# Order of the residual updates, of the feed-forward's down products and of three smaller pieces in a two-layer streaming encoder

## The chip, the cores and the metric

One core of one Trainium2 chip. The metric is the device time of one execution in microseconds (us). The kernel before took 3310.58 us, the median of three runs from 3303.72 to 3311.89.

## The reference, cut to what matters

Two requests run as one set of 1056 frames (1024 + 32) of width 1024 through two layers. Layer 0 mixes frames by retention and forgetting attention, layer 1 by a diagonal state space with a gate; in both, a cross-attention over 256 memory tokens and a feed-forward block follow. Each of the three branches stands between two norms:

```python
x = x + _rmsnorm(mix, g[1])
h = _rmsnorm(x, g[2])
mk, mv = _memory_kv(mem, mem_norm_w[layer], w_xk[layer], w_xv[layer])
x = x + _rmsnorm(_cross_attn(h, mk, mv, w_xq[layer], w_xo[layer]), g[3])
h = _rmsnorm(x, g[4])
x = x + _rmsnorm(_sq_relu_mlp(h, w_up[layer], w_down[layer]), g[5])

def _sq_relu_mlp(h, w_up, w_down):          # 1024 -> 4096 -> 1024
    return jnp.square(jax.nn.relu(h @ w_up)) @ w_down
```

## The kernel before

**Layout.** The width lies on the partitions as 8 tiles of 128; the frames are the free dimension, cut into groups 0, 1 and 2 of 384, 384 and 288 columns. Every large product is three matmuls (`mm3`, L72 below it): each operand is split into a high and a low part, and high by high, low by high and high by low are summed. A weight block comes by a DMA on SyncE's queue into a raw tile `wst` (four buffers, L151), ScalarE rounds it to `wh` (L153), and VectorE takes the difference `wl` (L154); `wh` and `wl` have four buffers each, and one weight block takes one of each and two `wst`.

**Feed-forward (`mlp`).** Group 2 goes first, in four steps c: eight up blocks, then a down product into all 8 output tiles in four pairs, with two loads of `wdn` to a pair. Groups 0 and 1 follow in eight steps. Step 0 is plain. From step 1 on, `seven` forms the up product of both groups from seven products on sums of their columns; one call gives four hidden tiles, in the order `c11` (group 0), `c22` (group 1), `c12` (group 1), `c21` (group 0), and a step has two calls. I call the tiles of the second call in a step c11' to c21'. A hidden tile is written twice: its high part by ScalarE (L1379), its low part by GpSimd (L1380); for c12 and c21 VectorE makes the square first (L1527). `down` then opens two output tiles at a time: all hidden tiles but the last for the first output, the same for the second, and then the last hidden tile for both. `gather` adds each result to its sum (VectorE L1416, in step 0 ScalarE L1414). Hence the boundary between `seven` and `down` stands once in each of steps 1 to 7 of both layers: 14 places.

**Updates (`update`, L261).** The residual with its norms for one group is eight parts; part k loads the old residual into `xr` (SyncE L286, four buffers), scales and adds on VectorE (L288, L289), splits the new value into `xh` (ScalarE L215) and `xl` (VectorE L216), stores it, and sums squares (ScalarE L258, GpSimd L259). After the parts, `pre_scale` sums over the partitions by small matmuls (`a<-ones_c,acc`), and `pre_row` spreads the result.

**Order.** `_Order` (`po`) is a clock that advances with the matmuls as the program is written; `later(dt, fn)` runs fn when the clock has gone dt further. It does so with a lead of 300 in the scheduler's priority, so what it issues passes ahead of other work on each engine, within its dependences. After that each engine works strictly through its own queue. The updates of groups 0 and 1 after the cross-attention (`lax`) run beside group 2's step 0.

Of the kernel before, what the change touches and what calls it, by code (L numbers as in the profile page):

```python
# [31 lines left out]
class _Order:  # L32
# [5 lines left out]

    def later(self, dt, fn):
        heapq.heappush(self.q, (self.now + dt, self.n, fn))  # L40
        self.n += 1
# [5 lines left out]
    def step(self):  # L47
        due, _, fn = heapq.heappop(self.q)
        self.now = max(self.now, due)
        with self.first():  # L50
            fn()
# [12 lines left out]
def _body(tc, A):  # L64
# [21 lines left out]
    with es:  # L86
# [174 lines left out]
        def update(o, g, ys, acc, gpost, xres, xout, last=False, row=False, scale=1.0 / 1024, half=False, r=None, lax=False, late=False, rlate=False):  # L261
# [3 lines left out]
            R = []  # L265
            d1, d2, d3, d4, dp = (10.0, 8.0, 14.0, 8.0, 10.0) if lax else (L1, L2, 25.0 if rlate else L3, L4, PU[g])
            if last and not late:
# [4 lines left out]
            def post_scale():  # L272
                rc = rstd_cols(acc, 3, scale, half, r=None if r is None else r())
                po.later(d2, lambda: add(rc))

            def add(rc):
# [4 lines left out]
                def part(k):  # L281
# [17 lines left out]
                    if k < 7:  # L299
                        po.later(dp, lambda: part(k + 1))  # L300
                        return
# [3 lines left out]
                    if not last:  # L305
                        po.later(d3, lambda: pre_scale(acc2))

# [16 lines left out]
            def pre_scale(acc2):  # L324
                rc = rstd_cols(acc2, 3, 1.0 / 1024, tag="rc" if row else "rx", ps=ba())
                if row:
                    po.later(d4, lambda: pre_row(rc))
                else:
                    o["r"] = rc
# [5 lines left out]

            po.later(d1, post_scale)

# [36 lines left out]
        def memory_k(l, xg=0):  # L374
# [3 lines left out]
            for k in range(8):  # L378
                mt = npl.tile([128, 384], F32, tag="xr", bufs=4, name="mt")[:, :256]
                dma(mt, A["memt"][:, k, :])  # L380
                mh.append(xtile(xg, "mh")[:, :256])
                ml.append(xtile(xg, "ml")[:, :256])
                with tc.high_priority(offset=HQ):
                    split_to(mh[k], ml[k], mt, gall[:, 12 + l, k : k + 1])
# [987 lines left out]
        def mlp(l, X, out, done, gpre, xsrc, last):  # L1372
# [23 lines left out]

            def down(ws, H, os_, g):

                n = len(H)
                pss = [bank()[:, : NG[g]] for _ in os_]  # L1400
                for ks in (range(n - 1), (n - 1,)):
                    for o, ps in zip(os_, pss):
                        for k in ks:
                            wh, wl = ws[k // 4]
                            s = slice((k % 4) * 256 + (o % 2) * 128, (k % 4) * 256 + (o % 2) * 128 + 128)
                            mm3(ps, wh[:, s], wl[:, s], H[k][0], H[k][1], k == 0, k == n - 1)
                            po.tick()
# [14 lines left out]
            for c in range(4):  # L1422
# [8 lines left out]
                for s4 in range(4):  # L1431
                    ws = [wload(A["wdn"][l, 2 * c + j, s4], 4) for j in range(2)]
                    os_ = (2 * s4, 2 * s4 + 1)
# [124 lines left out]
            for c in range(8):  # L1558
# [15 lines left out]
                ws = [wload(A["wdn"][l, c, s], 4) for s in range(4)]  # L1574
                for g in (1, 0) if c == 0 else (0, 1):
                    acc = acc_tile(NG[g]) if c == 7 else None
                    for s4 in range(4):
                        os_ = (2 * s4, 2 * s4 + 1)
                        for o, ps in zip(os_, down([ws[s4]], H[g], os_, g)):
                            gather(Y[g], o, g, ps, c == 0, acc)  # L1580
# [73 lines left out]
        def s5_block(f, u):  # L1654
# [54 lines left out]
            def outputs(xg):  # L1709
# [17 lines left out]
        gemm(range(8), lambda b: wload(A["winc"][b], 8, HP if b < 2 else 0), lambda g, k: get(X, g)[k], evac_u, lambda at: 2 if at == 0 else 1,  # L1727
             post=lambda b, g: s5_block(b, uts.pop(b)) if un[b] == 3 else None, order=(2, 0, 1))
        mem = memory_k(1, 2)
# [177 lines left out]
```

## Time and profile before

| | us |
|---|---|
| median of three runs | 3310.58 |
| the profiled execution | 3306.95 |
| its span (first to last instruction) | 3305.0 |
| TensorE busy in the span | 3119.2 (94%) |
| VectorE, ScalarE, GpSimd busy | 1925.8, 1327.7, 924.7 |

The profile is one execution, on the hardware profiler. What TensorE lacks to the span is waits; a second loss does not show as idle time, matmuls that run at the lower of the clock's two levels after a wait. So a stage is read by its length, not by its busy time.

### The profile page before, as it was taken

The page shows a single profiled execution, that of the slowest core. Times are in us where ns is not written, and L with a number is a line of the kernel's source. Part 1 is how long each engine was busy: PE and PEld are TensorE (multiplying, and loading weights), DVE is VectorE, ACT ScalarE, POOL GpSimd, SP SyncE. Part 2 cuts the span into 40 slices and gives each one's busy share as a digit, 9 for nine tenths or more (in the row PEclk, how much of TensorE's full clock was granted, in tenths as well). Part 3 has the DMA queues.
Part 4 walks back from the last instruction along what each step waited for, and adds up shares of the span by engine and source line. Part 5 has one row for each costly group of instructions (what it writes and reads, how often), then busy time and mean ns, then how long its engine had stood idle before and what let it go on. Part 6 is the DMA issues. An engine that isn't in the chain of part 4 may idle for free.

```text
span 3305.0 us, 52896 instructions
## 1 busy us (share of the span) xinstructions
PE 3119.2 (94%) x19636; PEld 3009.1 (91%) x19636; DVE 1925.8 (58%) x3600; ACT 1327.7 (40%) x2801; POOL 924.7 (28%) x1182
## 2 busy tenths in 40 slices
PE   7999999998999899999999987998999899999997
PEld 7899986688999899999999887998999899999997
DVE  8853666527534756566657696217435656566565
ACT  5213344525435545433324334225435545333232
POOL 4873431216104313111114332005105212111114
PEclk9999999999999899999999898999999999999998
DMA  5462254124113655222213676214114654112113
GB/s 162 148 199 65 63 138 122 41 58 137 55 40 118 196 164 155 69 64 65 77 51 110 192 252 194 68 52 144 49 50 138 188 166 149 61 58 87 52 65 102
DMA packets 255271, 360.49 MB, mean 109 GB/s; under 512 B 42795, under 2 KB 144396, under 8 KB 254884
## 3 DMA queue, kind: packets, MB, share of 16 engines
q1 hardware_dynamic: 211222, 289.63, 28.9%
q10 hardware_dynamic: 35328, 41.83, 3.8%
q0 software_dynamic: 8464, 25.66, 2.3%
q8 instruction: 154, 2.52, 0.3%
q14 instruction: 103, 0.84, 0.1%
HBM read 294.75 MB, written 66.39 MB: 109 GB/s over the span
## 4 chain that ended last, share of the span: by engine, by line
PE 66%; DVE 7%; issue 3%; ACT 2%; POOL 2%; DMA 2%; SPq 0%; DVEq 0%; ACTq 0%; POOLq 0%
PE mm L72 59%; PE a L72 4%; PE b L72 1%; PE c L72 1%; DVE upd L289 1%; DVE upd L288 1%; POOL acc L259 1%; DVE xl L216 1%; DVE us L1527 1%; ACT wh L153 1%; PE b L76 1%; DVE wl L154 1%; POOL hm L1380 0%; DVE p L1692 0%; DVE VC L1695 0%
## 5 line engine op out<-in xcount | busy, mean ns | idle before, releaser
L72 PE MATMUL mm<-hm,wh 128*128 128x384 f32 (+1 forms) x3072 | 740.1, 326 | 33.2 <-ACT wh L153 10.4
L154 DVE TENSOR_TENSOR wl<-wst,wh 128x512 fp32r<-128x512 f32 (+1 forms) x648 | 465.5, 735 | 359.7 <-ACT wh L153 354.7
L72 PE MATMUL mm<-xh,wh 128*128 128x384 f32 x1664 | 580.9, 349 | 13.4 <-ACT mo L414 8.0
L72 PEld LDWEIGHTS mm<-hm,wh 128*128 128x128 f32 x3072 | 540.2, 190 | 42.5 <-ACT hm L1379 14.6
L72 PE MATMUL mm<-xl,wh 128*128 128x384 f32 x1664 | 567.3, 341 | 4.3 <-DVE xl L216 4.3
L72 PE MATMUL mm<-xh,wl 128*128 128x384 f32 x1664 | 566.1, 340 | 3.2 <-DVE wl L154 3.2
L153 ACT ACTIVATE wh<-wst 128x512 fp32r<-128x512 f32 (+1 forms) x648 | 390.5, 625 | 409.8 <-PE mm L72 332.6
L72 PE MATMUL mm<-hm,wl 128*128 128x384 f32 (+1 forms) x1536 | 499.0, 325 | 14.8 <-DVE wl L154 14.8
L72 PE MATMUL mm<-xc,wh 128*128 128x288 f32 (+1 forms) x2368 | 489.4, 302 | 14.6 <-DVE mo L395 8.3
L259 POOL TENSOR_TENSOR acc<-acc,sq 128x384 f32<-128x384 f32 (+2 forms) x259 | 276.7, 1074 | 483.8 <-ACT sq L258 477.4
L72 PEld LDWEIGHTS mm<-xc,wh 128*128 128x128 f32 x2368 | 387.7, 193 | 16.7 <-DVE mo L395 8.5
L72 PE MATMUL mm<-xc,wl 128*128 128x288 f32 (+1 forms) x1184 | 353.8, 299 | 3.8 <-DVE wl L154 3.8
L1380 POOL TENSOR_TENSOR hm<-us,hm 128x384 fp32r<-128x384 f32 x112 | 125.8, 1123 | 777.7 <-ACT hm L1379 752.1
L72 PEld LDWEIGHTS mm<-xh,wh 128*128 128x128 f32 x1664 | 318.3, 191 | 20.7 <-ACT mo L414 8.9
L72 PEld LDWEIGHTS mm<-xl,wh 128*128 128x128 f32 x1664 | 318.6, 191 | 5.9 <-DVE xl L216 5.9
L72 PEld LDWEIGHTS mm<-xh,wl 128*128 128x128 f32 x1664 | 317.8, 191 | 3.5 <-DVE wl L154 3.5
L72 PEld LDWEIGHTS mm<-hm,wl 128*128 128x128 f32 x1536 | 291.6, 190 | 16.0 <-DVE wl L154 16.0
L1496 ACT ACTIVATE wh<-wst 128x512 fp32r<-128x512 f32 x196 | 115.1, 625 | 418.2 <-PE mm L72 372.2
L1416 DVE TENSOR_TENSOR y<-y,mm 128x384 f32<-128x384 f32 x224 | 120.6, 554 | 232.5 <-PE mm L72 232.5
L72 PEld LDWEIGHTS mm<-xc,wl 128*128 128x128 f32 x1184 | 228.3, 193 | 4.3 <-DVE wl L154 4.3
L72 PE MATMUL mm<-T,wh 128*128 128x384 f32 x672 | 171.6, 336 | 0.0
L1497 DVE TENSOR_TENSOR wl<-wst,wh 128x512 fp32r<-128x512 f32 x196 | 136.4, 728 | 34.8 <-ACT wh L1496 34.8
(502 smaller groups left out, 5414.9 us busy)
## 6 DMA issues: line engine op xcount, KB each, us to landing
wst<-in_wup_dram SPq DMA_DIRECT2D x256, 256.0 KB
wst<-in_wdn_dram SPq DMA_DIRECT2D x256, 256.0 KB
xs<-upd ACTq DMA_DIRECT2D x80, 192.0 KB
xr<-xs SPq DMA_DIRECT2D x80, 192.0 KB
wst<-in_wab_dram SPq DMA_DIRECT2D x40, 256.0 KB
wst<-in_wxk_dram SPq DMA_DIRECT2D x32, 256.0 KB
wst<-in_wxv_dram SPq DMA_DIRECT2D x32, 256.0 KB
wst<-in_wxq_dram SPq DMA_DIRECT2D x32, 256.0 KB
```

The lines of the kernel that those rows point to most:

```text
L72: return nc.tensor.matmul(out, lhsT, rhs, **kw)
L76: return nc.tensor.transpose(out, src, idn)
L153: act(wh[:, s], st, AF.Copy)
L154: vtt(wl[:, s], st, wh[:, s].bitcast(F32), op=SUB)
L216: stt(l, src, gain, h.bitcast(F32), op0=MULT, op1=SUB)
L259: return gtt(acc[:, :n], acc[:, :n], sq[:, :n], op=ADD)
L288: stt(t, ys[k], gall[:, gpost, k : k + 1], ps[:, :n], op0=MULT, op1=MULT)
L289: (gtt if last and k % 2 or r and k < 2 or not r and (g == 2 and k % 4 == 1) else vtt)(t, t, xr, op=ADD)
L1380: gtt(lo, t, h.bitcast(F32), op=SUB)
L1416: vtt(Y[o], Y[o], ps, op=ADD)
L1496: act(wh[:, d], src, AF.Copy)
L1497: vtt(wl[:, d], src, wh[:, d].bitcast(F32), op=SUB)
```

## The change

1. `later` takes `lead`. The updates of groups 0 and 1 after the cross-attention are queued with `lead=False`: they still come at their time on the clock, but at no higher priority than the code around them. 2. Their delays change (parts every 9 instead of 10, the norm's two steps 20 and 12 after instead of 14 and 8). The norm of group 2 after the feed-forward (`late`) waits 25 and 12 instead of 5.1 and 2.7. 3. The loads of `wdn` of group 2's step 0 get a lead of 600, as its up blocks' loads have already. 4. From step 1 on, `down` takes group 1 before group 0, and for group 1 the hidden tile with index 2 (c12') last. 5. The eight tiles through which the memory tokens pass use seven buffers of three kinds instead of four of one. 6. The state-space layer's input product takes the groups in the order 2, 1, 0 instead of 2, 0, 1.

```diff
-    def later(self, dt, fn):
-        heapq.heappush(self.q, (self.now + dt, self.n, fn))
+    def later(self, dt, fn, lead=True):
+        heapq.heappush(self.q, (self.now + dt, self.n, fn, lead))
...
-        with self.first():
+        with self.first() if lead else nullcontext():
...
-            d1, d2, d3, d4, dp = (10.0, 8.0, 14.0, 8.0, 10.0) if lax else (L1, L2, 25.0 if rlate else L3, L4, PU[g])
+            d1, d2, d3, d4, dp = (10.0, 8.0, 20.0, 12.0, 9.0) if lax else (L1, L2, 25.0 if rlate or late else L3, 12.0 if late else L4, PU[g])
...
-                        po.later(dp, lambda: part(k + 1))
+                        po.later(dp, lambda: part(k + 1), not lax)
...
-                        po.later(d3, lambda: pre_scale(acc2))
+                        po.later(d3, lambda: pre_scale(acc2), not lax)
...
-                mt = npl.tile([128, 384], F32, tag="xr", bufs=4, name="mt")[:, :256]
+                tag, bufs = (("xr", 4), ("xr", 4), ("xr", 4), ("tmp", 2), ("tmp", 2), ("sqa", 2), ("sqa", 2), ("xr", 4))[k]
+                mt = npl.tile([128, 384], F32, tag=tag, bufs=bufs, name="mt")[:, :256]
...
-            def down(ws, H, os_, g):
+            def down(ws, H, os_, g, late=None):
...
+                order = [k for k in range(n) if k != late] + ([] if late is None else [late])
                 pss = [bank()[:, : NG[g]] for _ in os_]
-                for ks in (range(n - 1), (n - 1,)):
+                for ks in (order[:-1], order[-1:]):
...
-                            mm3(ps, wh[:, s], wl[:, s], H[k][0], H[k][1], k == 0, k == n - 1)
+                            mm3(ps, wh[:, s], wl[:, s], H[k][0], H[k][1], k == order[0], k == order[-1])
...
-                    ws = [wload(A["wdn"][l, 2 * c + j, s4], 4) for j in range(2)]
+                    with tc.high_priority(offset=2 * HP if c == 0 else 0):
+                        ws = [wload(A["wdn"][l, 2 * c + j, s4], 4) for j in range(2)]
...
-                for g in (1, 0) if c == 0 else (0, 1):
+                for g in (1, 0):
...
-                        for o, ps in zip(os_, down([ws[s4]], H[g], os_, g)):
+                        for o, ps in zip(os_, down([ws[s4]], H[g], os_, g, 2 if c and g == 1 else None)):
...
-             post=lambda b, g: s5_block(b, uts.pop(b)) if un[b] == 3 else None, order=(2, 0, 1))
+             post=lambda b, g: s5_block(b, uts.pop(b)) if un[b] == 3 else None, order=(2, 1, 0))
```

The line numbers of the changed kernel are one to three higher after each edit.

**Where the instructions go, first place: group 2's first down product in layer 0.** SyncE's queue, as a piece of the difference; `xr<-xs` with 384 columns is an update part's load for groups 0 and 1, `wst<-in_wdn` a down weight, `wst<-in_wup` an up weight:

```order
 L286 DMA xr<-xs_86 128x384
 L151 DMA wst<-in_wup_dram 128x512 x2
-L151 DMA wst<-in_wdn_dram 128x512 x7
+L151 DMA wst<-in_wdn_dram 128x512 x8
 L286 DMA xr<-xs_93 128x384
 L286 DMA xr<-xs_87 128x384
+L151 DMA wst<-in_wdn_dram 128x512 x2
 L286 DMA xr<-xs_94 128x384
+L151 DMA wst<-in_wdn_dram 128x512 x2
 L286 DMA xr<-xs_88 128x384
 L286 DMA xr<-xs_95 128x384
-L151 DMA wst<-in_wdn_dram 128x512
+L151 DMA wst<-in_wdn_dram 128x512 x4
```

All 16 halves of down weights now stand before the last five of the 16 residual loads, and these move in among the next step's up weights. In either layer fourteen `xr` loads stand behind the first eight halves, the last four of them group 2's own. On VectorE at the same place, of the kernel before (from the first `wl` after the last up block's hidden tile):

```order
L154 TENSOR_TENSOR wl<-wst,wh 128x512
L216 SCALAR_TENSOR_TENSOR xl<-upd,gall,xh 128x384
L289 TENSOR_TENSOR upd<-upd,xr 128x384
L216 SCALAR_TENSOR_TENSOR xl<-upd,gall,xh 128x384
L288 SCALAR_TENSOR_TENSOR upd<-y,gall,b 128x384 x2
L216 SCALAR_TENSOR_TENSOR xl<-upd,gall,xh 128x384
L289 TENSOR_TENSOR upd<-upd,xr 128x384 x2
L288 SCALAR_TENSOR_TENSOR upd<-y,gall,b 128x384 x2
L216 SCALAR_TENSOR_TENSOR xl<-upd,gall,xh 128x384
L289 TENSOR_TENSOR upd<-upd,xr 128x384 x2
L216 SCALAR_TENSOR_TENSOR xl<-upd,gall,xh 128x384
L154 TENSOR_TENSOR wl<-wst,wh 128x512
```

and of the kernel changed, the fifth to the seventh of the eight down blocks:

```order
L154 TENSOR_TENSOR wl<-wst,wh 128x512 x2
L216 SCALAR_TENSOR_TENSOR xl<-upd,gall,xh 128x384
L154 TENSOR_TENSOR wl<-wst,wh 128x512 x2
L289 TENSOR_TENSOR upd<-upd,xr 128x384
L288 SCALAR_TENSOR_TENSOR upd<-y,gall,b 128x384
L216 SCALAR_TENSOR_TENSOR xl<-upd,gall,xh 128x384
L289 TENSOR_TENSOR upd<-upd,xr 128x384
L288 SCALAR_TENSOR_TENSOR upd<-y,gall,b 128x384
L216 SCALAR_TENSOR_TENSOR xl<-upd,gall,xh 128x384
L154 TENSOR_TENSOR wl<-wst,wh 128x512 x2
L289 TENSOR_TENSOR upd<-upd,xr 128x384
L288 SCALAR_TENSOR_TENSOR upd<-y,gall,b 128x384
```

Before, 14 update instructions stood between two single halves of a weight block; now at most six stand between two whole blocks. From the last up block's hidden tile on, the changed queue has 21 update instructions and 8 halves of down weights (four blocks) up to the first up weight of the next step, and then 9 update instructions and 8 halves to the end of that step's fourth up block.

**Second place: the first pair of outputs in a step after `seven`.** TensorE, layer 0, step 1, the second output's first three hidden tiles and then the first output's last one. In the order in which they are made, the hidden tiles are 15815 (c11), 15868 (c22), 15888 (c12), 15908 (c21), 15978 (c11'), 16031 (c22'), 16051 (c12') and 16071 (c21'), each with its low part one number higher. Before:

```order
L72 MATMUL mm_16116<-hm_15815,wh_16075 128x384
L72 MATMUL mm_16116<-hm_15816,wh_16075 128x384
L72 MATMUL mm_16116<-hm_15815,wl_16076 128x384
L72 MATMUL mm_16116<-hm_15908,wh_16075 128x384
L72 MATMUL mm_16116<-hm_15909,wh_16075 128x384
L72 MATMUL mm_16116<-hm_15908,wl_16076 128x384
L72 MATMUL mm_16116<-hm_15978,wh_16075 128x384
L72 MATMUL mm_16116<-hm_15979,wh_16075 128x384
L72 MATMUL mm_16116<-hm_15978,wl_16076 128x384
L72 MATMUL mm_16115<-hm_16071,wh_16075 128x384
L72 MATMUL mm_16115<-hm_16072,wh_16075 128x384
L72 MATMUL mm_16115<-hm_16071,wl_16076 128x384
```

and changed:

```order
L72 MATMUL mm_16116<-hm_15888,wh_16075 128x384
L72 MATMUL mm_16116<-hm_15889,wh_16075 128x384
L72 MATMUL mm_16116<-hm_15888,wl_16076 128x384
L72 MATMUL mm_16116<-hm_15868,wh_16075 128x384
L72 MATMUL mm_16116<-hm_15869,wh_16075 128x384
L72 MATMUL mm_16116<-hm_15868,wl_16076 128x384
L72 MATMUL mm_16116<-hm_16031,wh_16075 128x384
L72 MATMUL mm_16116<-hm_16032,wh_16075 128x384
L72 MATMUL mm_16116<-hm_16031,wl_16076 128x384
L72 MATMUL mm_16115<-hm_16051,wh_16075 128x384
L72 MATMUL mm_16115<-hm_16052,wh_16075 128x384
L72 MATMUL mm_16115<-hm_16051,wl_16076 128x384
```

The nineteenth matmul of the product needed c21', the last tile made; now it needs c12', the last but one, and the seventh needs c22' where it needed c11'.

**Third place: the norm of group 2 after its feed-forward in layer 0.** TensorE's rows around `pre_scale`, a piece of the difference; rows on `xh` are group 1's and 0's up product in step 0, rows on `hm` their down product:

```order
+L72 MATMUL mm<-hm,wl 128x384
+L72 MATMUL mm<-hm,wh 128x384 x2
+L72 MATMUL mm<-hm,wl 128x384
 L72 MATMUL a<-ones_c,acc 128x1 x3
-L72 MATMUL mm<-xh,wh 128x384
-L72 MATMUL mm<-xl,wh 128x384
-L72 MATMUL mm<-xh,wl 128x384
```

The three small matmuls moved from inside the up product to the down product that follows it.

## Rows read from the trace of the kernel before

**Rows 1.** The page: busy time of each engine; the chain that ended last, by engine.
```profile
PE 3119.2 (94%) x19636; PEld 3009.1 (91%) x19636; DVE 1925.8 (58%) x3600; ACT 1327.7 (40%) x2801; POOL 924.7 (28%) x1182
...
PE 66%; DVE 7%; issue 3%; ACT 2%; POOL 2%; DMA 2%; SPq 0%; DVEq 0%; ACTq 0%; POOLq 0%
```

**Rows 2.** Stages of layer 0: start, end, length, busy time of each engine.
```profile
core 0: us, PE busy (x) PEld busy (x) DVE busy (x) ACT busy (x) POOL busy (x), PEclk, DMA share, GB/s
1080.73:1123.26 42.53, 30.85 (x194) 30.04 (x193) 37.39 (x54) 24.83 (x51) 17.79 (x15) 0.80 0.69 214
1251.85:1277.30 25.45, 25.45 (x194) 25.45 (x193) 13.30 (x24) 11.98 (x24) 5.71 (x6) 1.00 0.49 160
1277.30:1319.86 42.56, 39.58 (x218) 39.21 (x217) 29.26 (x56) 25.53 (x56) 19.33 (x21) 0.92 0.52 152
1319.86:1353.43 33.57, 33.57 (x193) 33.57 (x193) 16.29 (x26) 16.51 (x36) 2.66 (x2) 1.00 0.23 71
1382.80:1418.30 35.50, 34.01 (x194) 33.43 (x193) 18.21 (x31) 5.56 (x10) 2.34 (x3) 1.00 0.17 53
```

**Rows 3.** The same columns, two stages of layer 1.
```profile
2557.70:2598.99 41.29, 27.70 (x194) 27.11 (x193) 36.75 (x53) 25.54 (x52) 17.31 (x15) 0.83 0.69 211
2753.04:2787.91 34.87, 34.87 (x207) 34.87 (x206) 24.18 (x45) 18.94 (x39) 14.32 (x15) 1.00 0.52 160
```

**Rows 4.** TensorE's waits, 1350 to 1800 us (total us, times, longest).
```profile
PE mm L72 <- POOL hm L1380: 5.1, 7, 1.1
PE mm L72 <- ACT hm L1379: 5.0, 7, 0.8
```

**Rows 5.** TensorE's waits, 2826 to 3282 us.
```profile
PE mm L72 <- ACT hm L1379: 5.2, 7, 0.8
```

**Rows 6.** TensorE in order of time around one boundary (start, length, line).
```profile
1512.54 0.51 PE L72 MATMUL mm<-hm,wh 128*128 128x384 f32 x2
...
1516.56 0.44 PE L72 MATMUL mm<-hm,wh 128*128 128x384 f32 x1 [0.74 <-ACT hm L1379]
1517.67 0.44 PE L72 MATMUL mm<-hm,wh 128*128 128x384 f32 x1 [0.67 <-POOL hm L1380]
```

**Rows 7.** ScalarE and GpSimd around the same boundary, two timelines.
```profile
1513.29 0.53 ACT L1379 ACTIVATE hm<-us 128x384 fp32r<-128x384 f32 x1 [1.11 <-DVE us L1527]
...
1511.73 1.11 POOL L1380 TENSOR_TENSOR hm<-us,hm 128x384 fp32r<-128x384 f32 x1 [5.09 <-ACT hm L1379]
1513.90 1.04 POOL L1380 TENSOR_TENSOR hm<-us,hm 128x384 fp32r<-128x384 f32 x1 [1.05 <-ACT hm L1379]
1516.58 1.03 POOL L1380 TENSOR_TENSOR hm<-us,hm 128x384 fp32r<-128x384 f32 x1 [1.65 <-ACT hm L1379]
```

**Rows 8.** TensorE's waits, 1080.73 to 1123.26 us, then 2557.7 to 2598.99.
```profile
PE mm L72 <- DVE wl L154: 11.7, 3, 5.5
...
PE mm L72 <- ACT wh L153: 10.4, 1, 10.4
```

**Rows 9.** Waits of SyncE's queue, 1075 to 1123 us.
```profile
SPq L286 <- DVE upd L289: 20.2, 11, 3.2
```

**Rows 10.** VectorE's groups, 1080.73 to 1123.26 us (count, busy us, mean ns).
```profile
L154 DVE TENSOR_TENSOR wl<-wst,wh 128x512 fp32r<-128x512 f32 x19 | 13.7, 731 | 5.1 <-ACT wh L153 5.0
L289 DVE TENSOR_TENSOR upd<-upd,xr 128x384 f32<-128x384 f32 x11 | 9.9, 915 | 0.0
```

**Rows 11.** VectorE's line 289, 1076 to 1109 us (min, median, max ns).
```profile
L289 DVE TENSOR_TENSOR upd<-upd,xr x14: 546/550/1376, 1076.6 to 1108.2; 128x384 f32<-128x384 f32 x14
```

**Rows 12.** GpSimd's sums, 1080.73 to 1123.26 us.
```profile
L259 POOL TENSOR_TENSOR acc<-acc,sq 128x384 f32<-128x384 f32 x13 | 15.6, 1214 | 19.5 <-ACT sq L258 19.5
```

**Rows 13.** TensorE's waits, 1277.3 to 1319.86 us.
```profile
PE a L72 <- POOL acc L259: 3.0, 1, 3.0
```

**Rows 14.** TensorE's waits, 1960 to 1992 us.
```profile
PE mm L72 <- DVE u L1651: 5.3, 2, 3.6
```

**Rows 15.** The start of the state-space layer, columns as in rows 2.
```profile
1797.00:1860.00 63.00, 51.35 (x264) 47.96 (x263) 48.34 (x78) 26.19 (x52) 38.06 (x38) 0.84 0.57 178
```

More of the change, by code (lines that the diff above doesn't have):

```diff
@@ L8 @@
 import heapq
-from contextlib import ExitStack
+from contextlib import ExitStack, nullcontext
 import numpy as np
@@ L47, in step @@
     def step(self):
-        due, _, fn = heapq.heappop(self.q)
+        due, _, fn, lead = heapq.heappop(self.q)
         self.now = max(self.now, due)
-        with self.first():
+        with self.first() if lead else nullcontext():
             fn()
@@ L273, in post_scale @@
                 rc = rstd_cols(acc, 3, scale, half, r=None if r is None else r())
-                po.later(d2, lambda: add(rc))
+                po.later(d2, lambda: add(rc), not lax)
             def add(rc):
@@ L326, in pre_scale @@
                 if row:
-                    po.later(d4, lambda: pre_row(rc))
+                    po.later(d4, lambda: pre_row(rc), not lax)
                 else:
@@ L334, in pre_row @@
                 act(o["r"], ps[:, :384], AF.Copy)
-            po.later(d1, post_scale)
+            po.later(d1, post_scale, not lax)
         def get(out, g, key="X"):
```

## The prediction

> **What bounds the kernel now.** I read the page first: TensorE is busy 94% of the span and is 66% of the chain that ended last [rows 1], so a change pays only where TensorE waits, or runs slowly after a wait. Then I cut TensorE's work into stages and compared stages that do the same products. The same 192 matmuls of group 2's down product take 25.45 us in its last step and 42.53 us in its first, where TensorE is busy only 30.85 us and the granted clock is 0.80, while VectorE is busy 37.39 us [rows 2]; in layer 1 the first takes 41.29 us [rows 3]. A down product of the 384-column groups takes 33.57 us in step 0 and 35.50 us in step 1 [rows 2]. The waits inside these stages come last: who released TensorE, and how long it stood.
>
> **The boundary after the seven products (edit 4).** The down product starts at 1512.54; TensorE then stands 0.74 us for ScalarE's high part of the last hidden tile and 0.67 us for GpSimd's low part of it [rows 6], which ends at 1516.58 + 1.03 = 1517.61 [rows 7]. The listed waits are 5.1 + 5.0 us for seven places in layer 0 [rows 4], and the row for layer 1 has seven more of the same kind [rows 5]: about 20 us in all. The stage tells more than the list, since a matmul that follows a wait also loses its overlap with the one before: 35.50 - 33.57 = 1.93 us a place [rows 2], 27.0 us for 14.
> In the new order the tile needed first, c22', has its low part ready at 1511.73 + 1.11 = 1512.84 [rows 7]. One matmul takes 33.57 / 192 = 0.175 us, so it is wanted after six matmuls, at 1512.54 + 6 x 0.175 = 1513.59: 0.75 us to spare. c12' is ready at 1513.29 + 0.53 = 1513.82 (high) and 1513.90 + 1.04 = 1514.94 (low) [rows 7], and wanted after 18, at 1515.69: 0.75 us again. c21' now serves group 0 alone, 96 matmuls or 16.8 us later. Nothing before the boundary is moved, so these times should hold. I take **-27**; the bounds are -20 (only the listed waits come back) and -27.
>
> **Group 2's first down product (edits 1, 2, 3).** TensorE stands 11.7 us there for `wl` in layer 0 and 10.4 us in one piece for `wh` in layer 1 [rows 8]; the rest of the loss is the low clock behind those waits (0.80 and 0.83 granted on average). Why are the weights late? On SyncE's queue the residual loads wait 20.2 us in 11 waits for an update's add to free a buffer [rows 9], and the down weights stand behind them; on VectorE 14 update instructions stand between two halves of weights. Against the undisturbed 25.45 us the stages lose 42.53 - 25.45 = 17.1 and 41.29 - 25.45 = 15.8 us, together 32.9.
> The change puts all down weights ahead on both queues, but the work stays. VectorE's instructions in this stage take 37.39 / 54 = 0.69 us each, collisions included [rows 2]. In its new queue, 29 stand between the end of the up blocks and the first weights of the next step: 20.1 us against 25.45. With the 17 behind them it is 46, or 31.8 us, up to the fourth up block, which TensorE reaches at 25.45 + 3 x 3.2 = 35.0 us (an up block being an eighth of a like stage, 25.45 / 8). So VectorE fits with 3 to 5 us over, not more, and every time it waits for a freed buffer comes off that. ScalarE's 24.83 us of work in this stage [rows 2] nearly fill 25.45 too. I leave 4 us of loss in each layer, between none and half of the present one (about 8), and take **-25** (33 - 8); the bounds are -16 and -33.
>
> **Group 2's norm after its feed-forward (edit 2).** In layer 0 the three small matmuls stand inside step 0's up product and wait 3.0 us for GpSimd's sum [rows 13]; the clock falls after it, 0.92 on average. That stage takes 42.56 us, the same one in layer 1, where this norm does not exist, 34.87 [rows 2, 3]. The 7.7 us between hold the norm's own matmuls, which only move: three sums and three spreads, estimated at 1.4 us from the 218 - 207 = 11 more instructions by about 0.13 us (25.45 / 194). By the new place, more than 70 matmuls into the down product, the sum is long done. **-6.3**, bounds -3 and -7.7.
>
> **Memory tiles (edit 5).** The loads come earlier and their splits move ahead of `u` on VectorE, where TensorE already stands 5.3 us in two waits [rows 14]. One to three splits of about 0.6 us delay the second: **+1.5**, bounds 0 and +4. **State-space order (edit 6).** It only swaps two like groups where TensorE has 63.00 - 51.35 = 11.65 us idle and VectorE is busy 48.34 [rows 15]; each of several waits can move by a part of itself. **0**, bounds -3 and +3.
>
> **Sum.** -27 - 25 - 6.3 + 1.5 = -56.8 against the profiled execution's 3306.95 us gives 3250.2. That execution lies 3.6 us under the median of the runs, so for the median I say **3254 us**.
>
> **A rule against this change.** VectorE's line 289 takes 0.55 us at the median, yet 1.376 at most [rows 11], 0.915 on average in the stage [rows 10], while GpSimd runs 13 sums of 1.214 us there [rows 12]. By these rows the collisions cost 11 x (0.915 - 0.55) = 4.0 us on this line, and with the 19 `wl` at 0.731 [rows 10] they are inside the 0.69 us that I used.
> The Trainium skill, page "SBUF — State Buffer", section "SBUF: two separate sides", says that VectorE and GpSimd share one pair of ports as an exclusive lock, held for a whole instruction, and that a VectorE instruction with two inputs there fully blocks meanwhile. By that rule 13 sums pressed into a shorter stage cost VectorE up to 13 x 1.214 = 15.8 us, and the stage would hardly shrink. The longest row, 0.83 us above the median, agrees with a block by most of a GpSimd instruction; the average does not agree with a block at every one.
>
> **Rivals.** *VectorE stays the bound.* If its 37.39 and 36.75 us of work [rows 2, 3] all have to be done inside the stage, as the collisions that this rule names would have it, the losses stay 11.9 and 11.3 us, only 9.7 of 32.9 is won, and the time is 3254 + 15 = 3269. For it speaks that it was busy nearly throughout; against it, that the weights now come first and that updates can slide into the next step, whose like stage keeps VectorE busy 13.30 of 25.45 us. *The boundary wait moves on.* The margin of c12' is 0.75 us, and VectorE, ScalarE and GpSimd make it one after another; if it slips by 1.5 us, half of edit 4's gain goes: 3254 + 13 = 3267. Against it: 14 alike places, no new work ahead of them. *Slower: residual loads dam up SyncE's queue.* In each layer 14 of them now stand among down and up weights, and a load that waits for its buffer holds every weight behind it. At the 1.84 us that such a wait takes on average now (20.2 / 11) and with nothing to hide it, 28 cost 51.5 us instead of the present 32.9, and the time is 3307 - 32 + 18.6 = 3294, or 3297 for the median; at the longest wait, 3.2 us, 89.6, and it is 3332 (3335). From 64.7 / 28 = 2.3 us a load the kernel is slower than before. Against it: four blocks of weights are kept ahead, worth 4 x 3.2 = 12.7 us of matmuls. *Nothing is gained* if the waits named are only where an earlier delay shows and TensorE is held later by the same amount: 3307 to 3310. Nothing in the stages behind, which run at full clock without waits, speaks for that.
>
> **How the numbers follow.** The forecast has 0.62, VectorE as the bound 0.16, the boundary's wait 0.10, little or no gain 0.06, the dammed queue 0.06 (0.04 slower than before, 0.02 about the same). The predicted time is the forecast's. The low end takes every lower bound, -27 - 33 - 7.7 + 0 - 3 = -70.7, thus 3240; the high end takes both middle rivals at once, 3254 + 15 + 13 = 3282; 4 us more each way are for the spread of the three runs (8 us), which gives 3236 to 3286. That leaves out about 0.12 at the top and a little below. The forecast's own range is 3243 to 3266. A measurement of this kernel tells 0.3%, about 10 us, from no change: faster 0.62 + 0.16 + 0.10 = 0.88, same 0.08, slower 0.04.
>
> **What would show it.** The 14 stages after `seven` at 33.6 us with no wait on `hm`; group 2's first down products at 28 to 32 us with a granted clock near 1 and no `xr` load's wait ahead of a `wdn`; step 0's up product in layer 0 at about 35 us, with no wait for `acc`; the two waits for `u` a little longer. I am wrong if VectorE runs without a break through the first down product and TensorE still waits for `wl`; if waits for the high or low part of c12' stand at the boundary; or if the up blocks of group 2's second step begin to wait for weights.

## The result, and the profile after

The changed kernel takes 3253.43 us, the median of four runs (3251.18 to 3262.17); beside it the kernel before took 3311.23 us (four runs, 3303.72 to 3316.42). The ratio is 0.9832, with a 95% interval from 0.9806 to 0.9858: 1.7% faster, 57.8 us between the two medians. The profiled execution took 3254.24 us, its span 3252.5 us, 52.5 us less than before.

Stages first, in the columns of [rows 2]. Layer 0 of the changed kernel: group 2's first down product, the up and down product of its next step, step 0's up and down product of groups 0 and 1, and the down product of step 1.

```profile
1079.29:1106.06 26.77, 25.97 (x194) 25.50 (x193) 26.77 (x43) 19.62 (x42) 13.39 (x10) 1.00 0.81 254
1106.06:1131.79 25.73, 25.73 (x194) 25.51 (x193) 22.80 (x34) 17.96 (x39) 11.82 (x12) 1.00 0.75 241
1131.79:1158.31 26.52, 26.38 (x200) 26.15 (x199) 14.81 (x28) 11.35 (x22) 3.63 (x5) 1.00 0.55 178
1260.80:1296.55 35.75, 35.05 (x206) 34.73 (x205) 24.19 (x45) 20.12 (x44) 16.83 (x19) 1.00 0.50 142
1296.55:1338.54 41.99, 38.10 (x205) 37.27 (x205) 21.49 (x37) 22.36 (x47) 5.00 (x4) 0.92 0.29 90
1367.91:1401.48 33.57, 33.57 (x193) 33.57 (x193) 18.09 (x31) 5.56 (x10) 2.37 (x3) 1.00 0.18 57
```

Layer 1: group 2's first down product, and step 0's up and down product of groups 0 and 1.

```profile
2529.48:2556.42 26.94, 25.73 (x195) 25.50 (x193) 26.94 (x42) 19.29 (x42) 14.28 (x11) 1.00 0.81 261
2712.58:2747.44 34.86, 34.86 (x206) 34.86 (x205) 22.99 (x44) 18.18 (x38) 14.32 (x15) 1.00 0.49 153
2747.44:2787.14 39.70, 35.88 (x194) 34.94 (x193) 20.01 (x34) 21.19 (x44) 5.97 (x3) 0.96 0.28 88
```

Group 2's first down product went from 42.53 to 26.77 us and from 41.29 to 26.94, at full clock. The boundary stage went from 35.50 to 33.57, the length without any wait. Step 0's up product in layer 0 went from 42.56 to 35.75, as forecast; but the down product behind it, 33.57 us before, now takes 41.99 at a clock of 0.92. That row is the miss.

The waits of TensorE, as total, times and longest; first over all boundaries of layer 0 (1340 to 1772 us, where [rows 4] had 14 waits on `hm`):

```profile
PE mm L72 <- DVE y L1418: 0.8, 1, 0.8
```

None of the 14 is left; the one row is the last step's sum. In layer 1 (2787 to 3229 us) the same view lists nothing. Then group 2's first down product in layer 0, which answers to [rows 8]:

```profile
PE mm L72 <- ACT yc L1416: 0.7, 1, 0.7
```

and in layer 1:

```profile
PE mm L72 <- ACT yc L1416: 1.2, 1, 1.2
```

The waits for weights are gone, 11.7 and 10.4 us of them in [rows 8]; what is left waits for ScalarE to read a product out of PSUM. Then step 0's down product in layer 0:

```profile
PE mm L72 <- ACT u L1386: 3.1, 1, 3.1
PE mm L72 <- ACT y L1416: 0.8, 1, 0.8
```

and the stretch of the state-space layer where TensorE waits for `u`:

```profile
PE mm L72 <- DVE u L1654: 6.7, 2, 6.2
```

This answers to [rows 14]: 5.3 us became 6.7. SyncE's queue in the 32 us around group 2's first down product, beside [rows 9]:

```profile
SPq L286 <- DVE upd L289: 10.0, 7, 2.3
...
SPq L151 <- DVE wl L154: 10.6, 16, 2.3
```

The residual loads still wait, 10.0 us in 7 waits (to the end of the next up product 10.9 us in 8; in layer 1, from 2524 to 2586 us, 11.7 us in 8), but the weights that TensorE needs next are no longer behind them.

The account of the profiled span, from the first matmul of each stage to that of the next (us):

| stretch | before | after | difference |
|---|---|---|---|
| up to layer 0's feed-forward | 1052.6 | 1051.1 | -1.4 |
| group 2's first down product and the next step, layer 0 | 94.1 | 79.0 | -15.1 |
| the same, layer 1 | 92.9 | 80.6 | -12.2 |
| step 0 of groups 0 and 1, up and down, layer 0 | 76.1 | 77.7 | +1.6 |
| the same, layer 1 | 73.2 | 74.6 | +1.3 |
| steps 1 to 6, both layers (12 boundaries) | | | -23.0 |
| layer 1's last down product | 37.0 | 35.1 | -1.9 |
| layer 0's last down product to layer 1's feed-forward | 757.7 | 755.9 | -1.8 |

### The profile page after: what moved, and what is told of

Same layout as the page of the kernel before. It is cut to its first block, busy times and chain, and to the rows that moved or that the text cites. A ratio compares the mean times of both kernels' runs of the same rounds, so it can differ in the third digit from the quotient of the medians.

```text
span 3252.5 us, 52906 instructions
## 1 busy us (share of the span) xinstructions
PE 3107.3 (96%) x19636; PEld 3003.3 (92%) x19636; DVE 1924.5 (59%) x3600; ACT 1324.5 (41%) x2801; POOL 938.8 (29%) x1182
## 4 chain that ended last, share of the span: by engine, by line
PE 65%; DVE 6%; DMA 4%; issue 3%; ACT 2%; POOL 2%; SPq 0%; ACTq 0%; DVEq 0%; POOLq 0%
PE mm L72 58%; PE a L72 4%; PE b L72 1%; PE c L72 1%; DVE wl L154 1%; DVE upd L289 1%; POOL acc L259 1%; DVE xl L216 1%; DVE upd L288 1%; PE b L76 1%; DMA wst<-in_wxv_dram 1%; DMA yf<-yd 1%; DMA wst<-in_wup_dram 1%; DMA xs<-upd 0%; DMA xq<-xs 0%
## 5 line engine op out<-in xcount | busy, mean ns | idle before, releaser
L259 POOL TENSOR_TENSOR acc<-acc,sq 128x384 f32<-128x384 f32 (+2 forms) x259 | 283.4, 1100 | 489.9 <-ACT sq L258 483.5
```

What stands on the lines that cost most here:

```text
L259: return gtt(acc[:, :n], acc[:, :n], sq[:, :n], op=ADD)
```

## The experiments

Each is a kernel of its own, made from the kernel before or from the changed one by the edit shown. The lengths are of stages, from one profile each, counted from the first matmul of a stage to the first of the next. Where no wait stands they repeat far better than whole times, which differ by up to 16 us between runs of one kernel (edit 4 alone: 3280.41 to 3296.43).

**Edit 4 alone.** The kernel before with this and the reordered `down`:

```diff
-                for g in (1, 0) if c == 0 else (0, 1):
+                for g in (1, 0):
...
-                        for o, ps in zip(os_, down([ws[s4]], H[g], os_, g)):
+                        for o, ps in zip(os_, down([ws[s4]], H[g], os_, g, 2 if c and g == 1 else None)):
```

> The kernel before with edit 4 alone (group 1 first, c12' last). My theory: the 12 undisturbed stages after the seven products fall from 35.5 to 33.57 us, the time by 26 us to about 3285, and everything else stays, the 42.5 and 41.3 us of group 2's first down products too. Rival: half of the 52 us that the whole change gave needs the other edits as well (a shared queue), and this alone gives under 15 us.

Measured: 3285.12 us (3309.24 beside it), ratio 0.9935, 0.9915 to 0.9954. The 12 stages are at 33.57 us, group 2's first down products at 42.55 and 41.08, and the time is the forecast one. The rival falls: this term stands by itself.

**Edits 1 and 3, and edit 2 for groups 0 and 1.** The kernel before with the new `later`, the new delays of `lax` and the lead of the down weights.

```diff
-        with self.first():
+        with self.first() if lead else nullcontext():
...
-(10.0, 8.0, 14.0, 8.0, 10.0) if lax
+(10.0, 8.0, 20.0, 12.0, 9.0) if lax
...
+                    with tc.high_priority(offset=2 * HP if c == 0 else 0):
```

> The kernel before with edit 1, edit 2 for groups 0 and 1 and edit 3 (updates without lead, later norms, down weights of group 2's first step ahead), and nothing else. My theory: group 2's first down products at 27 us instead of 42.5 and 41.3, 27 us gained after what the next stages give back, about 3284 us; the wait of group 2's norm (3.0 us for the sum) is still there. Rival: without the other edits the updates' leftovers push the next stages by more than 3 us.

Measured: 3278.33 us, ratio 0.9917, 0.9895 to 0.9939. The first down products take 27.91 and 27.42 us, with the next step 80.2 and 80.8 us instead of 94.1 and 92.9: 26 us. The two stages behind them grow by 0.7 and 1.8 us, less than the rival's 3. The time is 6 us under the expected 3284, of which 3.6 us lie ahead of layer 0's feed-forward (1049.0 us instead of 1052.6), where a single profile tells little. The two parts, 26 and 26 us, make up nearly the whole of the 52.5 us between the profiles.

**Edit 3 alone, and edits 1 and 2 alone.** The same kernel split in two:

```diff
# the first: edit 3, nothing else
+                    with tc.high_priority(offset=2 * HP if c == 0 else 0):
# the second: edits 1 and 2 for groups 0 and 1, nothing else
+        with self.first() if lead else nullcontext():
...
+(10.0, 8.0, 20.0, 12.0, 9.0) if lax
```

> The kernel before with edit 3 alone: the down weights of group 2's first step get a lead of 600, the updates keep theirs of 300 and the old delays. My theory: weights late on SyncE's queue and on VectorE are the whole cause, so this alone brings the first down products to 27 to 29 us; the updates then crowd behind them and the two stages that follow (25.5 and 26.1 us) give back 1 to 4 us a layer. Rival: the lead of the updates is the cause; then the down products stay above 35 us.

> The kernel before with edit 1 and edit 2 for groups 0 and 1, without edit 3. My theory: down weights still stand behind single residual loads, no longer behind five or more; the first down products take 28 to 33 us, so either edit alone brings over half of the gain. Rival: both edits are needed, and the stages stay above 36 us.

Measured: 3286.78 and 3284.04 us, one run each. With the lead of the weights alone, in the columns of [rows 2], the first down product and the up product behind it:

```profile
1073.20:1105.26 32.06, 25.86 (x195) 25.40 (x193) 31.96 (x49) 20.93 (x46) 16.91 (x14) 1.00 0.77 246
1105.26:1134.66 29.40, 28.37 (x193) 28.02 (x193) 20.56 (x31) 17.82 (x37) 8.30 (x9) 0.88 0.61 199
```

and TensorE's waits over the two:

```profile
PE mm L72 <- ACT wh L153: 5.0, 1, 5.0
...
PE mm L72 <- DVE wl L154: 1.0, 1, 1.0
```

The down weights come in time. The wait has moved to the first up weight of the next step, which has no lead and queues behind the updates: 5.0 us, counted at the end of the 32.06 us, and the clock of the stage behind it falls to 0.88. Only 6.5 and 5.4 us are won in the two layers. With no lead for the updates and none for the weights either, the first two stages are:

```profile
1087.18:1114.04 26.86, 25.71 (x194) 25.47 (x193) 26.31 (x41) 19.79 (x41) 11.22 (x11) 1.00 0.82 254
1114.04:1140.07 26.03, 25.73 (x195) 25.49 (x194) 22.88 (x35) 18.32 (x41) 13.78 (x11) 1.00 0.71 237
```

That is the whole gain, 15.1 and 13.2 us with the down product behind; adding edit 3 to it, as in the run above, brings nothing that shows. Both of my expectations were off: I had put the cause on the place of the down weights, and it is the way the updates are queued, which push back whatever weights come next. Which part of that counts, the lost lead (edit 1) or the new delays (edit 2), is not shown: no run has one without the other. The rivals "both are needed" and "above 35 us" fall too.

**The later norm undone.** The changed kernel with

```diff
-25.0 if rlate or late else L3, 12.0 if late else L4
+25.0 if rlate else L3, L4
```

> The changed kernel with group 2's norm after its feed-forward early again (5.1 and 2.7 instead of 25 and 12). My theory of the miss: the later norm only uncovers a wait behind it, ScalarE's work on the column sums of groups 0 and 1, which step 0's up and down products of layer 0 run into. Then with the early norm the up product is back at 42 us and the down product behind it at about 34, the two together within 2 us of the 77.7 us of the changed kernel, and the time is 3252 to 3255 us. Rival: the down product is late for another reason and stays at 42 us; then the two take 84 us and the time is 3260.

Measured: 3255.14 us, ratio to before 0.9839, 0.9814 to 0.9865, against 0.9832 for the changed kernel: no difference. Step 0's up and down product, layer 0:

```profile
1263.67:1305.23 41.56, 38.35 (x219) 37.70 (x217) 30.47 (x56) 25.74 (x55) 18.56 (x21) 0.96 0.51 155
1305.23:1338.80 33.57, 33.57 (x194) 33.57 (x193) 16.30 (x26) 16.59 (x36) 2.07 (x2) 1.00 0.22 70
```

Together 75.1 us, 2.6 under the changed kernel's 77.7, a little outside the 2 us that I had allowed. Over all profiles the sign stays open: the six kernels with the early norm take 74.7 to 76.3 us for the two stages, the changed kernel and the two made from it that touch nothing here (the next two runs) 77.7, 76.9 and 74.0. So the later norm brings no gain that shows. In each of the six the down product takes 33.57 us, in all eight kernels with the later norm 39.1 to 42.0, of which the norm's own matmuls are about 1.4.

**Group 1 first, c22' last.** The changed kernel with

```diff
-down([ws[s4]], H[g], os_, g, 2 if c and g == 1 else None)
+down([ws[s4]], H[g], os_, g, None)
```

> The changed kernel with group 1 first, but its hidden tiles in their own order (c22' last instead of c12'). My theory: c12' is then wanted by the seventh matmul, 1.05 us after the start, and its low part ready 2.4 us after it, so TensorE waits for ScalarE and GpSimd again, 1.2 to 1.6 us in all, and the 14 stages take 34.9 to 35.3 us: about 20 us more in all. Rival: the order of the groups does all of it, and the stages stay at 33.57.

Measured: 3273.39 us (one run), the stages 34.88 to 34.96 us, 1.3 us above the changed kernel's. TensorE waits for the low part of c12':

```profile
PE mm L72 <- POOL hm L1381: 4.0, 6, 0.7
```

and at one of the boundaries, in order of time:

```profile
1433.91 0.45 PE L72 MATMUL mm<-hm,wh 128*128 128x384 f32 x1 [0.64 <-POOL hm L1381]
```

0.64 us are listed, 1.33 us are lost, as at the old boundary, where 1.41 listed were 1.93 lost. Of edit 4's 1.93 us the groups' order brings 0.6 and the tiles' order 1.3.

**VectorE's first instruction of each update part issued twice.**

```diff
+                    for _ in range(2 if lax else 1):
-                    stt(t, ys[k], gall[:, gpost, k : k + 1], ps[:, :n], op0=MULT, op1=MULT)
+                        stt(t, ys[k], gall[:, gpost, k : k + 1], ps[:, :n], op0=MULT, op1=MULT)
```

> The changed kernel with the first VectorE instruction of each update part of groups 0 and 1 after the cross-attention issued twice (the same result is written twice), about 0.55 to 0.6 us more for each of the 16 parts of a layer. My theory: VectorE has 3 to 5 us over in group 2's first down product and the blocks behind it, so 9 us more come out as 3 to 6 us in a layer, spread over the first down product (26.8 and 26.9 us), and the up and down products of the next step (25.7 and 26.5; 27.1 and 26.6). Rival one: VectorE is the bound already, and all 9 us come out. Rival two: ScalarE is the bound, VectorE has more room than I worked out, and less than 1.5 us comes out.

Measured: 3252.39 us (one run). The three stages, in the columns of [rows 2]:

```profile
1075.76:1101.21 25.45, 25.45 (x195) 25.45 (x193) 25.45 (x43) 18.95 (x40) 13.87 (x9) 1.00 0.82 253
1101.21:1126.67 25.46, 25.46 (x195) 25.46 (x193) 25.46 (x42) 17.41 (x37) 12.38 (x10) 1.00 0.72 234
1126.67:1158.57 31.90, 28.69 (x201) 27.80 (x199) 18.79 (x34) 13.63 (x26) 6.13 (x7) 0.95 0.53 175
```

82.8 us instead of 79.0, in layer 1 84.1 instead of 80.6: 3.8 and 3.5 us, as expected, but all of it at the third stage. The doubled line itself takes 8.9 us more in layer 0 (18.4 instead of 9.5), VectorE as a whole is busy 6.4 us more over these stages and the one ahead of them (91.2 instead of 84.8; 5.6 in layer 1), since the 64 `wl` come out shorter (736 ns on average instead of 772). VectorE is busy without a break through the first two stages, which lose nothing at all; the debt is called in at the next down product, where TensorE waits 1.8 and 1.4 us for the two parts of hidden tiles. In the whole time this does not show: the profile has other stages 2 to 4 us shorter than the changed kernel's.

**Four tries at step 0's down product.** The changed kernel with a lead for the hidden tiles of step 0, with it and one of two additions, and with the sums without lead:

```diff
# first
-H[g].append(hidden(up(ws[b], get(X, g), g), NG[g]))
+ps = up(ws[b], get(X, g), g)
+with tc.high_priority(offset=2 * HP):
+    H[g].append(hidden(ps, NG[g]))
# second: the sums alone
-po.later(1.0 + 9.0 * k, lambda k=k: sums(k))
+po.later(1.0 + 9.0 * k, lambda k=k: sums(k), False)
# third: the first, and
+po.later(1.0 + 13.0 * k, lambda k=k: sums(k))
# fourth: the first, and in gather
+with tc.high_priority(offset=HP):
+    act(Y[o], ps, AF.Copy)
```

> The changed kernel with a lead of 600 for the hidden tiles of groups 0 and 1 in step 0 (reading the product from PSUM, squaring, splitting), ahead of the column sums for the seven products, which have 300. My theory of the missed term: ScalarE reaches the last hidden tiles late because it does the column sums first, so step 0's down products (42.0 us in layer 0, 39.7 in layer 1, against 33.6 without waits) lose their first wait and with it the low clock, and fall to 36 to 38 us in layer 0 and 37 to 39 in layer 1; the time falls by 4 to 7 us to about 3248. Rival: ScalarE has too much to do in this stretch whatever its order; the wait moves to the sums or to the first step after, and nothing is gained.

> The changed kernel with the column sums for the seven products queued without lead (same times on the clock, no higher priority than the code around them), as edit 1 did for the updates. My theory: ScalarE then reads the products of step 0 out of PSUM first, and the down products fall to 35 to 37 us in both layers (from 42.0 and 39.7), with the sums still done before the first of the seven products. Rival: the sums come too late, and the stage of the first seven products (29.36 us) grows by what the down products lose.

> The changed kernel with the lead of 600 for step 0's hidden tiles and the column sums 13 instead of 9 apart on the clock. My theory: ScalarE's load in the stretch falls by a third, the last of the two waits (for the first sums that are read out of PSUM, 1.6 and 2.1 us with the lead alone) falls below 1 us, and the down products take 35 to 37 us. Rival as for the plain sums: the first seven products wait instead.

> The changed kernel with the lead of 600 for step 0's hidden tiles and as much for reading the first down products out of PSUM. My theory: both waits are matters of order on ScalarE alone, so both fall below 1 us, and the down products take 35 to 37 us in both layers. Rival: ScalarE's instructions ahead of them wait for VectorE and for loads themselves, order alone does not help, and the stages stay at 39 us as with the first lead alone.

Step 0's up and down product, and the medians (us; one run where no ratio stands):

| | layer 0 | layer 1 | time | ratio to before |
|---|---|---|---|---|
| before | 42.56 + 33.57 | 34.87 + 38.35 | 3310.58 | |
| changed | 35.75 + 41.99 | 34.86 + 39.70 | 3253.43 | 0.9832 (0.9806 to 0.9858) |
| hidden tiles lead | 34.86 + 39.32 | 34.86 + 39.29 | 3252.91 | 0.9819 (0.9803 to 0.9836) |
| sums without lead | 34.86 + 41.26 | 34.85 + 38.64 | 3265.69 | |
| hidden tiles lead, sums 13 apart | 34.86 + 39.23 | 34.86 + 38.32 | 3248.93 | |
| hidden tiles and gather lead | 34.86 + 39.47 | 34.86 + 39.32 | 3253.13 | |

With the lead layer 0's two stages are 3.6 us shorter than in the changed kernel's profile, layer 1's 0.4. That this is the lead's doing is not shown: the doubled instruction above, without any lead here, has 34.86 + 39.12 us in layer 0, also at full clock. All four miss what was expected of the down products (36 to 39 us of the first, 35 to 37 of the others), and no order that I tried gets below 38. The first seven products stay at 29.36 us in all four, so no sum came too late. With the first lead alone, two waits of 1.8 and 1.6 us stay:

```profile
1301.49 0.62 PE L72 MATMUL mm<-hm,wh 128*128 128x384 f32 x2 [1.81 <-ACT u L1386]
...
1304.91 0.62 PE L72 MATMUL mm<-hm,wh 128*128 128x384 f32 x2 [1.57 <-ACT y L1416]
```

On ScalarE the last hidden tile's read (`u<-mm`, L1386) stands behind pieces of the column sums (L1461, L212), the first of which waits for its load, and a weight:

```profile
1299.10 0.62 ACT L1461 ACTIVATE xq<-xq,gall 128x384 f32<-128x384 f32 x1 [0.70 <-DMA xq<-xs]
1299.62 0.51 ACT L212 ACTIVATE T<-xd 128x384 fp32r<-128x384 f32 x1
1300.04 0.61 ACT L153 ACTIVATE wh<-wst 128x512 fp32r<-128x512 f32 x1
1300.56 0.51 ACT L212 ACTIVATE T<-xd 128x384 fp32r<-128x384 f32 x1
1300.97 0.47 ACT L1386 ACTIVATE u<-mm 128x384 f32<-128x384 f32 x1
```

The stages of the last run came out as its rival said, at 39 us. That the reason is work which stands ahead of the late read and waits for loads itself is read from this one trace, not tested. The plain sums' 3265.69 us is not theirs: that run reached the feed-forward at 1062.4 us instead of 1051.1.

**The third of these tries, without edit 3.** The kernel with the hidden tiles' lead and the sums 13 apart, without the lead of the down weights:

```diff
-                    with tc.high_priority(offset=2 * HP if c == 0 else 0):
-                        ws = [wload(A["wdn"][l, 2 * c + j, s4], 4) for j in range(2)]
+                    ws = [wload(A["wdn"][l, 2 * c + j, s4], 4) for j in range(2)]
```

> The changed kernel with the lead for step 0's hidden tiles and the column sums 13 apart, as in the run with both, and without edit 3 (group 2's first down weights have no lead of their own). My theory: with the updates queued without lead the down weights need none, so group 2's first down product and the two stages behind it take 78.5 to 80.5 us in layer 0 and 79 to 81 in layer 1, as in the changed kernel (79.0 and 80.6), step 0's down products 38 to 39.5, and the time is 3246 to 3252 us, some 0.1 to 0.2% under the changed kernel. Rival: within the whole change the lead of the down weights is worth something, and these three stages take 3 us or more longer.

Measured: 3255.77 us (five runs, 3247.48 to 3260.95), ratio 0.9836, 0.9814 to 0.9858: the changed kernel again, and my interval missed. Step 0's down products take 40.25 and 38.22 us, where 38 to 39.5 was expected. The three stages of group 2 take 79.6 us in layer 0, as expected, but 83.4 in layer 1, after a wait of 3.1 us for ScalarE and a low stretch of the clock behind it. Whether edit 3 is worth these 3 us stays open: the same three stages of layer 1 differ from 80.0 to 82.4 us between the changed kernel and six made from it that all have edit 3 and change nothing there. Nothing that I tried beats the changed kernel by a measurable amount.

## Why the prediction was right, and where it was not

**The sum.** 3254 us was forecast, 3253.43 measured; against its own profile the forecast was -56.8 us, and the profiles differ by 52.7. The boundary came 1 us short, the first down product 2.3 us over, the norm's 6.3 us did not come, and the stretches put at nothing or at +1.5 made up part of it. Against the profile the forecast was 4 us too low. That it meets the median within 1 us is luck: 3.6 us were added because the old profile lay under its median, and the new one lies 0.8 us above its own.

**The boundary (-27).** Right in mechanism and size: 14 places, 1.93 us at twelve of them and at the last of layer 1, about 1 us at the last of layer 0, 26 us in all. Edit 4 alone shows it, and the run with c22' last shows that the times of the tiles were read rightly: c12' wanted at the seventh matmul costs 1.3 us, wanted at the nineteenth nothing. The rule that a stage tells more than its listed waits held again.

**Group 2's first down product (-25).** 27.3 us came, inside the bounds. The size was right, but the step that names the cause was not: "the change puts all down weights ahead on both queues". That by itself, edit 3 alone, is worth 12 us, since the wait comes back at the next up weight; the new queueing of the updates (edits 1 and 2) brings all of it without edit 3. What the prediction should have priced is how the updates stand among the weights, not the place of the 16 loads. That VectorE has something over, estimated at 3 to 5 us a layer, is borne out by the doubled instruction: 8.9 us more on its line cost 3.8 in layer 0, so 5 were over by this line; by VectorE's whole busy time, 6.4 and 5.6 us more for 3.8 and 3.5, it is 2 to 3. VectorE is busy without a break through the first down product (26.77 of 26.77 us), the first half of what I had named as a sign of error; the second half, a wait for `wl`, is not there. The up blocks of the second step do not wait for weights either: they take 25.73 us, and in layer 1 27.13, with two short waits for `u` (0.4 and 0.7 us).

**VectorE as the bound, and the page's rule.** The rival asked that the 37.39 us stay in the stage. They did not: 26.77 us are done there, and the up product behind it, where VectorE was busy 13.08 us before (1123.26 to 1148.72 us), has 22.80. VectorE's time for one instruction fell to 26.77 / 43 = 0.62 us, from 0.69, but collisions did not cease. GpSimd runs 8 sums in the stage instead of 13, each longer, 1.474 us instead of 1.214; on VectorE the add became shorter, 617 ns on average instead of 915 [rows 10], but `wl` longer, 816 instead of 731, and so did `xl`. Before:

```profile
L216 DVE SCALAR_TENSOR_TENSOR xl<-upd,gall,xh 128x384 fp32r<-128x384 f32 x13 | 10.1, 778 | 0.0
```

and changed, on VectorE and GpSimd (1079.29 to 1106.06 us):

```profile
L154 DVE TENSOR_TENSOR wl<-wst,wh 128x512 fp32r<-128x512 f32 x15 | 11.7, 816 | 0.0
L216 DVE SCALAR_TENSOR_TENSOR xl<-upd,gall,xh 128x384 fp32r<-128x384 f32 x9 | 8.2, 916 | 0.0
L289 DVE TENSOR_TENSOR upd<-upd,xr 128x384 f32<-128x384 f32 x9 | 5.6, 617 | 0.0
...
L259 POOL TENSOR_TENSOR acc<-acc,sq 128x384 f32<-128x384 f32 x8 | 11.7, 1474 | 12.4 <-ACT sq L258 12.4
```

From 1074 to 1120 us line 289 now has

```profile
L289 DVE TENSOR_TENSOR upd<-upd,xr x14: 546/547/1172, 1076.3 to 1113.9; 128x384 f32<-128x384 f32 x14
```

The Trainium skill, page "SBUF — State Buffer", section "SBUF: two separate sides", was cited for a block of a whole GpSimd instruction. Single rows still agree with it (the longest 1.172 us, the median 0.547). The stage that it would have kept long became short all the same: the GpSimd work thinned out with the updates, 11.7 us of sums instead of 15.6, instead of being pressed together.

**Group 2's norm (-6.3).** It did not come: step 0 of layer 0 takes 1.6 us more, and over all the kernels no gain shows. The wait for `acc` went, the up product fell by 6.8 us, both as said. What failed is the step that let the gain stand: "Nothing in the stages behind, which run at full clock without waits, speaks for that", that TensorE is held later instead. The down product behind ran without waits because ScalarE caught up during the 3 us stall and the low clock. Before, ScalarE reads the last of step 0's eight products at once after the down product's start at 1319.86:

```profile
1320.21 0.48 ACT L1385 ACTIVATE u<-mm 128x384 f32<-128x384 f32 x1
```

Once TensorE comes on time, ScalarE still has column sums before it (its timeline):

```profile
1302.53 0.52 ACT L212 ACTIVATE xh<-xd 128x384 fp32r<-128x384 f32 x1 [0.71 <-DVE xd L1467]
1302.96 0.60 ACT L1461 ACTIVATE xq<-xq,gall 128x384 f32<-128x384 f32 x1
1303.46 0.47 ACT L1386 ACTIVATE u<-mm 128x384 f32<-128x384 f32 x1
```

and TensorE's timeline at that point:

```profile
1303.98 0.63 PE L72 MATMUL mm<-hm,wh 128*128 128x384 f32 x2 [3.10 <-ACT u L1386]
...
1307.31 1.01 PE L72 MATMUL mm<-hm,wh 128*128 128x384 f32 x2 [0.79 <-ACT y L1416]
```

The read `u<-mm`, the last of eight, starts 6.9 us after the down product's start at 1296.55, and TensorE waits 3.1 us for it. So it is in all the kernels: that read starts 0.4 to 1.0 us after the down product's start in the six with the early norm, 5.2 to 6.9 us in the eight with the later one, and 4.2 to 6.1 us in layer 1 of all fourteen. The profile before had this on show, in the same stage of layer 1, where that norm does not exist:

```profile
2787.91:2826.26 38.35, 35.60 (x194) 34.96 (x194) 19.41 (x34) 20.42 (x43) 2.71 (x2) 0.96 0.27 84
```

38.35 us instead of 33.57, at a clock of 0.96. I took layer 1's up product as the measure of layer 0's and did not take the down product beside it. With both, the term is 76.13 - 73.22 = 2.9 us, and without the 1.4 us of the norm's own matmuls about 1.5.

**Memory tiles and the state-space order (+1.5 and 0).** The waits for `u` grew by 1.4 us as forecast. In the whole stretch from layer 0's last down product to layer 1's feed-forward the +1.5 can't be told: 754.8 to 758.1 us in the nine profiles with these two edits, 756.6 to 762.5 in the five without, and edit 4, which all nine have, takes 1 us off its first stage.

**The dammed queue, the rival on the slower side.** It did not come: SyncE's residual loads wait 10.0 us in 7 waits, 1.4 us each, under the 2.3 from which it would have decided, and no weight that TensorE waits for stands behind them.

## What to carry to other kernels

Work that has time to spare should not carry a lead: the two updates were pushed ahead by priority, and each weight behind them, whichever it was, was late; taking the lead away (here together with new delays) was worth more than giving one to the weights. Before a stall is counted as gain, look at the same stretch in another layer that lacks the stall, and at the stage behind it: whoever was late there uses the stall to catch up. At a boundary, order the consumer by when its operands are finished, group by group and tile by tile: 0.75 us of margin was enough at all 14 places.

## What the runs showed that I had not expected

The same wait can cost different amounts. With group 2's norm in its old place, step 0's up product in layer 0 has a wait of 2.9 to 3.0 us for `acc`. Of the six kernels with it three take 42.5 to 42.7 us for the stage and three 41.1 to 41.6, and the granted clock over it is 0.92 in the first three (before: [rows 2]) and 0.96 in the other three, though the wait is the same. What decides between the two is open. With the later norm the two stages of step 0 together take 74.0 to 77.7 us in three kernels that do not differ there. So a difference of 1 us in the one, or of 3 us in the other, says nothing of an edit.

Up to layer 0's feed-forward, where these kernels differ in little but the memory tiles, the fourteen profiles take between 1045.1 us (edit 3 alone) and 1062.4 us (the sums without lead). A single time is therefore no measure for an edit of a few us; the stages, which repeat to a hundredth where no wait stands (33.57 us, 29.36 us), are.
